# A hybrid RWKV-7 decoder step on one core: the scaled key turned by transfers instead of identity products, and four groups of operations scheduled with priority

## The chip, the core and the metric

The kernel runs on one core of a Trainium2 chip. TensorE (PE in the profile) multiplies matrices into PSUM; its weight loads (PEld) overlap its products. VectorE (DVE), ScalarE (ACT) and GpSimd (POOL) do the rest of the arithmetic, and SyncE (SP) issues most of the transfers. Each engine takes its instructions in order, and an instruction that waits holds what is behind it on that engine. The metric is the device time of one execution in microseconds; lower is better.

## The reference

One layer of a decoder trunk, for 1024 prompt tokens and 8 sequences of 8 sample tokens (1088 columns in all), model width 1024, 8 heads of 64:

```python
h = rms_norm(x, norm_mix) * (1 + sc) + sh
P = h @ w_in                                  # 4352 columns: RWKV, pooling, two gates
def step(S, inp):                             # one token of the RWKV-7 state, per head
    r_t, w_t, k_t, v_t, kk_t, a_t = inp
    sa = einsum("bhvk,bhk->bhv", S, -kk_t)
    S = S * w_t + sa[..., None] * (kk_t * a_t) + v_t[..., None] * k_t
    return S, einsum("bhvk,bhk->bhv", S, r_t)
merged = sigmoid(g_r) * (o_r @ w_br_rwkv) + sigmoid(g_p) * (o_p @ w_br_pool)
x = x + gt * (merged @ w_out)
x = x + gt2 * (square(relu(h2 @ w_ff1)) @ w_ff2)
y = rms_norm(x, norm_final)
```

## The kernel before

Features lie on the partitions, tokens along the free dimension. The wide products are made of float32 operands split in two: a high half (`hi`, float32r) and the rest (`lo`), and three products, hi by hi, hi by lo and lo by hi (`mm3`, L415), stand for one.

**Weights.** `weights` (L391) asks SP for 128x512 floats (`wraw`, two buffers), ScalarE rounds them to `whi`, DVE takes the difference `wlo`; `whi` and `wlo` have two buffers each (four in the second part). From its 68th call on, every other difference is GpSimd's. `products` (L439) issues a job's products, calls `load` for the half of a block that comes two later (L466), and at a job's end hands its three PSUM banks to `consume` (L473): the dense eviction, ScalarE's copy into `px` for the columns of `w_in`, DVE's operations for `w_br` and `w_out`.

**The RWKV units.** The heads are taken in four pairs. `front` (L808) makes decays, keys and sums of a pair on DVE and ScalarE. The 1024 prompt tokens are 16 chunks of 64, in units 0 and 1 of eight chunks each; unit 2 holds the sample tokens. `ra` (L888) makes two halves of a unit's tile `ra`: `ra[:, :, 1, :]` is the scaled key, minus `kk` times the decay, and `ra[:, :, 0, :]` the scaled receptance. For unit 0 `front` calls it (L876), for the others `unit` (L929). `unit` (L919) makes the scores (products `bk` by `ra`, masked by DVE into `ab[..., 0:64]` and `at`), scales the sums `bk`, brings the value rows by eight transfers of 32x32 blocks (`swap`, L1008, and a DVE transpose into `uv`), turns the scaled key by 16 products with the identity into a PSUM bank that DVE copies into `at[:, :, 0, :]` (L978 to L988), and turns the scaled sums into `ab[..., 64:128]` by TensorE and ScalarE (L992 to L998). `inverse`, `level` and `affine` solve the triangular systems of a pair; `affine` is the first to read `at[:, :, 0, :]`. `chain` (L1140) then runs through the 16 chunks: two products add to a bank, DVE makes the next state `S` out of it (L1164), two more products follow.

**The order.** TensorE's order is fixed when the program is made. `Pace` runs the wide products as background (`stream`) and puts the generators `chains`, `heads`, `pools` and `or_rows` between them; each yields a condition (`need`: operands and a bank are ready by the model of the other engines in `Clocks`, whose L142 prices an operation by its size; `room`: DVE's backlog is short) and runs on when it holds. The order of the other engines, SP's issues among them, is made at the build by a list scheduler that simulates the program: of the instructions whose operands are ready it takes the one earliest in the program. Transfers of `swap` and `weights` go through SP alike.

The second part (`phase2`, L1524) has `w_br`, `w_out` and the MLP, whose weights go through `pair` (L1518) with other buffers.

Of the kernel before, what the change touches and what calls it, by code (L numbers as in the profile page):

```python
# [9 lines left out]
F32 = mybir.dt.float32  # L10
F32R = mybir.dt.float32r
BF16 = mybir.dt.bfloat16
AF = mybir.ActivationFunctionType
ALU = mybir.AluOpType
# [307 lines left out]
class K:  # L322
# [68 lines left out]
    def weights(self, src):  # L391

        nc = self.nc
        n = self.nw
        self.nw += 1
        wp, x = (self.p2, "x") if self.deep and n % 4 > 1 else (self.wp, "")
        raw = self.wp.tile([P, 512], F32, tag="wraw", bufs=WB[0], name=self.nm("wraw"))
        nc.sync.dma_start(raw, src)
        hi = wp.tile([P, 512], F32R, tag="whi" + x, bufs=WB[1], name=self.nm("whi"))
        lo = wp.tile([P, 512], F32R, tag="wlo" + x, bufs=WB[1], name=self.nm("wlo"))  # L400
        nc.scalar.activation(hi, raw, AF.Copy)
        (nc.gpsimd if n % 2 and n >= self.solo else nc.vector).tensor_tensor(lo, raw, hi.bitcast(F32), op=ALU.subtract)
        return [(hi[:, q * 128:(q + 1) * 128], lo[:, q * 128:(q + 1) * 128]) for q in range(4)]

    def split(self, t, src):
# [33 lines left out]
    def products(self, flat, W, load):  # L439
        for j, h, *qs in flat:  # L440
            if isinstance(j, Unit):
                yield from j.go(W.pop((id(j), h)))
                load()
                if j.after:
                    j.after()
                continue
            if not isinstance(j, Job):
                yield from j()
                continue
            if h == 0 and (not qs or qs[0] == 0):  # L450
                if not j.hold:
                    j.consume = j.begin()
                j.pss = [self.ps(t) for _, t in zip(j.chunks, j.tags)]
            w = W[id(j), h]
            if not qs or qs[-1] == 3:
                del W[id(j), h]
            last = len(j.halves) - 1
            xh, xl = j.xs()
            for q in qs or range(4):
                for (c0, n), ps in zip(j.chunks, j.pss):  # L460
                    self.mm3(ps[:, :n], w[q], col(xh[4 * h + q], c0, n), col(xl[4 * h + q], c0, n),
                             h == 0 and q == 0, h == last and q == 3)
                    yield
            if qs and qs[-1] < 3:
                continue
            load()  # L466
            if h == last:
                if j.hold:
                    while j.hold not in self.done:
                        yield "idle"  # L470
                    j.consume = j.begin()
                for (c0, n), ps in zip(j.chunks, j.pss):
                    j.consume(c0, n, ps)  # L473
                if j.after:
                    j.after()

# [411 lines left out]
    def ra(self, d, u):  # L888
# [2 lines left out]
        C = 8 if u < 2 else 1  # L891
        cs = slice(8 * u, 8 * u + C)
        ra = self.p1.tile([P, C, 2, 64], F32, tag=f"ra{C}", bufs=2 if u < 2 else 1, name=self.nm("ra"))
        d["qs"][u] = dict(ra=ra)
        if u < 2:
            nc.vector.scalar_tensor_tensor(ra[:, :, 1, :], cut(kk[:, :NPR])[:, cs], -1.0, ev[:, cs, 0:64], op0=ALU.mult, op1=ALU.mult)
            nc.vector.tensor_tensor(ra[:, :, 0, :], cut(r[:, :NPR])[:, cs], ev[:, cs, 1:65], op=ALU.mult)
        else:
            nc.vector.scalar_tensor_tensor(cut8(ra[:, 0, 1, :]), cut8(kk[:, NPR:NT]), -1.0, es[:, :, 0:8], op0=ALU.mult, op1=ALU.mult)
# [19 lines left out]
    def unit(self, f, d, u):  # L919
# [8 lines left out]
        if u:  # L928
            self.ra(d, u)  # L929
        tl = lambda tag, shape, n=2: self.p1.tile([P, C] + shape, F32, tag=f"{tag}{C}", bufs=n if prompt else 1, name=self.nm(tag))  # L930
        Q = dict(ab=tl("ab", [2, 128]), uv=tl("uv", [2, 64]), ra=d["qs"][u]["ra"])
        d["qs"][u] = Q
        ra, ab, uv = Q["ra"], Q["ab"], Q["uv"]
        if prompt:
            at = Q["at"] = tl("at", [2, 64])
# [39 lines left out]
        if prompt:  # L975
            for h, hs in enumerate(HB):
                nc.vector.transpose(uv[hs, :, h, :], rest[h])
        yield self.need(ra, *[] if prompt else [v[:, NPR:NT]])  # L978
        ps = self.ps("w")
        for i in range(C):  # L980
            for h, hs in enumerate(HB):
                os = HB[1 - h]
                if prompt:
                    self.mm(ps[os, i * 64:(i + 1) * 64], ra[hs, i, 1, :], ident[hs, hs], start=True, stop=True, tile_position=(hs.start, os.start))
                else:
                    self.mm(ps[hs, 0:64], v[hs, NPR:NT], ident[hs, hs], start=True, stop=True)
        if prompt:
            nc.vector.tensor_copy(at[:, :, 0, :], cut(ps))  # L988
        else:
            for h, hs in enumerate(HB):  # L990
                nc.scalar.activation(uv[hs, 0, h, :], ps[hs, 0:64], AF.Copy)
        for a in range(0, C, 4):  # L992
# [147 lines left out]
    def chain(self, f, d):  # L1140
# [4 lines left out]
        for u in range(2):  # L1145
# [9 lines left out]
            for i in range(8):  # L1155
# [5 lines left out]
                else:  # L1161
                    for hs in HB:
                        self.mm(pn[hs, at], ra[hs, i, 1, :], S[hs, :], start=False, stop=True, skip_group_check=True)
                    nc.vector.scalar_tensor_tensor(S1, S, end[:, c:c + 1], pn[:, at], op0=ALU.mult, op1=ALU.add)  # L1164
                    for hs in HB:
                        self.mm(py[hs, at], S[hs, :], ra[hs, i, 0, :], start=False, stop=True, skip_group_check=True)
                S = S1
# [920 lines left out]
def cut(t):  # L2088
    return t.rearrange("p (c j) -> p c j", j=64)
# [90 lines left out]
```

## Time and profile before

| | |
|---|---|
| runs shown | 1601.74 and 1603.80 us, median 1602.77 us |
| profiled execution | 1604.23 us, of which 1602.4 us from the first to the last instruction |
| PE, DVE, ACT, POOL busy | 96%, 69%, 41%, 9% of the span |
| mean granted TensorE clock | 0.99 |
| transfers | 290.32 MB, 181 GB/s |

The page cuts the span into 40 slices of 40 us; a digit is the busy share of a slice in tenths (9 is 90% or more), PEclk the clock that the throttle granted:

```profile
PE   4999999999998999999999999999999999999997
PEld 2898888988898879989998999999999999999997
DVE  4575758776876487547542697998767796666774
ACT  4454354455334544522222572222334344344651
```

The first slice holds the first loads and the norm; up to about 775 us run `w_in`, the RWKV units and the pooling branch, behind that `w_br`, `w_out` and the MLP. A matmul of the profile has a modelled end, so a TensorE that is busy all the time is not one at its peak. A row of the waits reads: engine, tile and line that waited, what it waited for, us in total, times, longest. In a row of the timeline the bracket at the end is the idle time of the engine just before the instruction, and what ended it; L187 and L358 are the helpers that record every operation of DVE, ACT, POOL and SP, and every product, so the tiles' names tell what a row is (`kct` holds the identity).

### The profile page before, as it was taken

The numbers are of one execution on the slowest core, as the hardware profiler recorded it, in microseconds if no ns is written. First come the engines' busy times: TensorE is split into PE (matmuls) and PEld (weight loads), VectorE is DVE, ScalarE is ACT, GpSimd is POOL, SyncE is SP. The second block draws the span as 40 slices with busy tenths as digits, with TensorE's granted clock in tenths as the row PEclk, the third lists the DMA queues.
The fourth block names the chain that finished last, engine by engine and source line by source line (L and its number), as shares of the span: only waits on it lengthen the run. The fifth ranks groups of instructions, "written<-read, shape, count | busy, mean of one in ns | idle before, by whom it ended". The sixth has DMA issues, their size and how long they took to land.

```text
span 1602.4 us, 34165 instructions
## 1 busy us (share of the span) xinstructions
PE 1544.8 (96%) x13851; PEld 1453.6 (91%) x13851; DVE 1097.8 (69%) x1932; ACT 662.7 (41%) x1286; POOL 139.1 (9%) x220
## 2 busy tenths in 40 slices
PE   4999999999998999999999999999999999999997
PEld 2898888988898879989998999999999999999997
DVE  4575758776876487547542697998767796666774
ACT  4454354455334544522222572222334344344651
POOL 0100100000000000012500120000000050000000
PEclk9999999999999999999999999999999999999999
DMA  9242523234333343855884555665345996664753
GB/s 343 89 134 76 181 84 112 93 127 133 101 122 104 113 125 106 322 180 186 310 295 162 183 198 170 237 212 200 139 151 213 387 365 196 213 200 142 234 192 119
DMA packets 137438, 290.32 MB, mean 181 GB/s; under 512 B 37920, under 2 KB 42016, under 8 KB 137280
## 3 DMA queue, kind: packets, MB, share of 16 engines
q1 hardware_dynamic: 129856, 266.75, 48.4%
q10 hardware_dynamic: 5360, 14.26, 2.6%
q0 software_dynamic: 2064, 7.13, 1.3%
q8 instruction: 109, 1.79, 0.5%
q14 instruction: 49, 0.40, 0.1%
HBM read 210.80 MB, written 77.28 MB: 180 GB/s over the span
## 4 chain that ended last, share of the span: by engine, by line
PE 76%; DVE 6%; DMA 4%; issue 2%; ACT 1%; SPq 1%; DVEq 0%; ACTq 0%
PE mm L358 50%; PE w L358 13%; PE wc L358 12%; DVE wt L187 1%; DVE hx L187 1%; DMA mg<-in_w_ff 1%; DMA wt<-d_x 1%; SPq L187 1%; DMA hid<-in_w_ada_mlp 1%; DVE wlo L187 1%; DMA hid<-in_w_ff 1%; PE w L389 0%; DVE hv L187 0%; ACT wt L187 0%; DMA uv<-d_x 0%
## 5 line engine op out<-in xcount | busy, mean ns | idle before, releaser
L358 PE MATMUL mm<-hx,whi 128*128 128x362 f32 (+2 forms) x2944 | 689.9, 322 | 6.4 <-ACT px L187 3.7
L358 PEld LDWEIGHTS mm<-hx,whi 128*128 128x128 f32 x2944 | 497.3, 190 | 29.2 <-issue 11.5
L358 PE MATMUL mm<-hx,wlo 128*128 128x362 f32 (+2 forms) x1472 | 463.7, 315 | 5.8 <-DVE wlo L187 5.8
L358 PEld LDWEIGHTS mm<-hx,wlo 128*128 128x128 f32 x1472 | 279.5, 190 | 6.6 <-DVE wlo L187 6.6
L358 PE MATMUL mm<-mg,whi 128*128 128x272 f32 (+2 forms) x1312 | 249.5, 289 | 0.5 <-DVE t L187 0.5
L358 PEld LDWEIGHTS mm<-mg,whi 128*128 128x128 f32 x1312 | 205.4, 188 | 5.1 <-issue 2.5
L358 PE MATMUL mm<-mg,wlo 128*128 128x272 f32 (+2 forms) x656 | 188.5, 287 | 0.0
L358 PE MATMUL wc<-hx,whi 128*128 128x272 f32 x896 | 170.4, 287 | 0.0
L358 PEld LDWEIGHTS wc<-hx,whi 128*128 128x128 f32 x896 | 140.3, 188 | 0.0
L187 ACT ACTIVATE whi<-hid 128x512 fp32r<-128x512 f32 x128 | 80.4, 630 | 144.6 <-PE mm L358 59.6
L358 PE MATMUL wc<-hx,wlo 128*128 128x272 f32 x448 | 128.9, 288 | 1.0 <-DVE wlo L187 1.0
L358 PEld LDWEIGHTS mm<-mg,wlo 128*128 128x128 f32 x656 | 123.5, 188 | 0.0
L187 DVE TENSOR_TENSOR wlo<-hid,whi 128x512 fp32r<-128x512 f32 x128 | 87.9, 688 | 48.5 <-ACT whi L187 47.9
L187 DVE TENSOR_TENSOR wlo<-wraw,whi 128x512 fp32r<-128x512 f32 x84 | 60.7, 724 | 68.1 <-ACT whi L187 64.6
L187 ACT ACTIVATE whi<-wraw 128x512 fp32r<-128x512 f32 x100 | 62.6, 627 | 94.0 <-PE mm L358 56.9
L358 PE MATMUL w<-hx,whi 128*128 128x272 f32 (+1 forms) x480 | 96.9, 296 | 0.0
L358 PEld LDWEIGHTS wc<-hx,wlo 128*128 128x128 f32 x448 | 84.2, 188 | 1.3 <-DVE wlo L187 1.2
L187 POOL TENSOR_TENSOR hx<-hx,rs 128x64 f32<-128x64 f32 x24 | 35.2, 1465 | 569.5 <-DMA mg<-in_w_ff 376.2
L358 PEld LDWEIGHTS mm<-mg,hx 128*128 128x128 f32 x576 | 72.9, 188 | 5.0 <-issue 5.0
L358 PEld LDWEIGHTS w<-hx,whi 128*128 128x128 f32 x480 | 77.0, 188 | 0.0
L358 PE MATMUL mm<-mg,hx 128*128 128x272 f32 (+2 forms) x576 | 75.5, 290 | 0.0
L187 ACT ACTIVATE px<-mm 128x362 f32<-128x362 f32 (+3 forms) x113 | 46.3, 435 | 60.7 <-PE mm L358 53.9
(275 smaller groups left out, 2312.7 us busy)
## 6 DMA issues: line engine op xcount, KB each, us to landing
t<-d_t SPq DMA_DIRECT2D x56, 544.0 KB, 4.9
hid<-in_w_ff SPq DMA_DIRECT2D x110, 256.0 KB, 3.8
d_t<-hx SPq DMA_DIRECT2D x102, 272.0 KB, 2.2
hid<-in_w_ff SPq DMA_DIRECT2D x42, 512.0 KB, 3.8
wraw<-in_w_in SPq DMA_DIRECT2D x68, 256.0 KB, 2.8
mg<-in_w_ff SPq DMA_DIRECT2D x58, 256.0 KB, 5.4
hid<-in_w_ada_mlp SPq DMA_DIRECT2D x24, 512.0 KB, 5.7
d_th<-px SPq DMA_DIRECT2D x22, 544.0 KB, 3.0
```

The lines of the kernel that those rows point to most:

```text
L187: return f(*a, **kw)
L358: return self.nc.tensor.matmul(out, lhsT, rhs, **kw)
```

## The change

The scaled key of units 0 and 1 is turned without TensorE. `ra` allocates the tile `ab` too, and as soon as the scaled key is made it asks SP for eight transfers (two calls of `swap`) that put its 32x32 blocks into their turned places in `ab[:, :, 0, 64:128]`, the halves of the partitions exchanged. Where `unit` had the 16 identity products, the wait ahead of them and DVE's copy out of PSUM, DVE now transposes within the blocks from there into `at[:, :, 0, :]`. ScalarE later writes the turned sums into the same columns of `ab`. Unit 2 keeps its products for the value rows.

Four groups of operations are put into a block `high_priority()`: the scheduler takes them ahead of all others as soon as their operands are ready. They are the two operations of the weights' splitting in `weights`, a job's evictions, and the state sum `S1` in `chain`. TensorE's order stands outside of this, and so do the loads' transfers.

```diff
@@ weights
-        nc.scalar.activation(hi, raw, AF.Copy)
-        (nc.gpsimd if n % 2 and n >= self.solo else nc.vector).tensor_tensor(lo, raw, hi.bitcast(F32), op=ALU.subtract)
+        with self.tc.high_priority():
+            nc.scalar.activation(hi, raw, AF.Copy)
+            (nc.gpsimd if n % 2 and n >= self.solo else nc.vector).tensor_tensor(lo, raw, hi.bitcast(F32), op=ALU.subtract)
@@ products
                 for (c0, n), ps in zip(j.chunks, j.pss):
-                    j.consume(c0, n, ps)
+                    with self.tc.high_priority():
+                        j.consume(c0, n, ps)
@@ ra
-        d["qs"][u] = dict(ra=ra)
+        ab = self.p1.tile([P, C, 2, 128], F32, tag=f"ab{C}", bufs=2 if u < 2 else 1, name=self.nm("ab"))
+        d["qs"][u] = dict(ra=ra, ab=ab)
         if u < 2:
             nc.vector.scalar_tensor_tensor(ra[:, :, 1, :], cut(kk[:, :NPR])[:, cs], -1.0, ev[:, cs, 0:64], op0=ALU.mult, op1=ALU.mult)
+            for h, hs in enumerate(HB):
+                self.swap(ab[HB[1 - h], :, 0, 64:128], ra[hs, :, 1, :])
             nc.vector.tensor_tensor(ra[:, :, 0, :], cut(r[:, :NPR])[:, cs], ev[:, cs, 1:65], op=ALU.mult)
@@ unit
-        Q = dict(ab=tl("ab", [2, 128]), uv=tl("uv", [2, 64]), ra=d["qs"][u]["ra"])
-        d["qs"][u] = Q
+        Q = d["qs"][u]
+        Q["uv"] = tl("uv", [2, 64])
...
-        yield self.need(ra, *[] if prompt else [v[:, NPR:NT]])
-        ps = self.ps("w")
-        for i in range(C):
+        if prompt:
+            nc.vector.transpose(at[:, :, 0, :], ab[:, :, 0, 64:128])
+        else:
+            yield self.need(v[:, NPR:NT])
+            ps = self.ps("w")
             for h, hs in enumerate(HB):
-                os = HB[1 - h]
-                if prompt:
-                    self.mm(ps[os, i * 64:(i + 1) * 64], ra[hs, i, 1, :], ident[hs, hs], start=True, stop=True, tile_position=(hs.start, os.start))
-                else:
-                    self.mm(ps[hs, 0:64], v[hs, NPR:NT], ident[hs, hs], start=True, stop=True)
-        if prompt:
-            nc.vector.tensor_copy(at[:, :, 0, :], cut(ps))
-        else:
+                self.mm(ps[hs, 0:64], v[hs, NPR:NT], ident[hs, hs], start=True, stop=True)
             for h, hs in enumerate(HB):
                 nc.scalar.activation(uv[hs, 0, h, :], ps[hs, 0:64], AF.Copy)
@@ chain
-                    nc.vector.scalar_tensor_tensor(S1, S, end[:, c:c + 1], pn[:, at], op0=ALU.mult, op1=ALU.add)
+                    with self.tc.high_priority():
+                        nc.vector.scalar_tensor_tensor(S1, S, end[:, c:c + 1], pn[:, at], op0=ALU.mult, op1=ALU.add)
```

## The prediction, made before the changed kernel was run

> **What bounds the kernel now.** I read the page's busy shares first, then the busy table over three stretches, then TensorE's waits from 30 to 775 us, which is the part with the RWKV units.
>
> ```profile
> PE 1544.8 (96%) x13851; PEld 1453.6 (91%) x13851; DVE 1097.8 (69%) x1932; ACT 662.7 (41%) x1286; POOL 139.1 (9%) x220
> ```
> ```profile
> 30.00:775.00 745.00, 719.25 (x7351) 646.73 (x7344) 502.45 (x905) 329.17 (x674) 67.46 (x144) 0.98 0.42 139
> 775.00:1602.40 827.40, 815.63 (x6460) 800.75 (x6458) 583.75 (x1012) 318.96 (x596) 68.81 (x61) 1.00 0.62 214
> ```
> ```profile
> PE wc L358 <- DVE S L187: 6.4, 5, 2.8
> PE mm L358 <- DVE wlo L187: 5.2, 2, 3.4
> PE mm L358 <- ACT px L187: 3.7, 3, 3.1
> ...
> PE mm L358 <- DVE px L187: 1.4, 1, 1.4
> ```
>
> TensorE (PE) sets the time in both parts: what is taken off its work, or off its waits, is taken off the end. (The columns after the length are busy time of PE, weight load, DVE, ACT and POOL, then the granted clock.) Between 30 and 775 us it is idle for 745.0 - 719.3 = 25.8 us, and 16.7 of that are these four rows (total, times, longest). After 775 us it is idle for 11.8 of 827.4 us; of the changed lines only the weights of `w_br` and `w_out` and their evictions work there. I take nothing there, and look for the whole effect in the first part.
>
> The granted clock makes a wait dearer than its row says. These are the first part's stretches of low clock:
>
> ```profile
> 123.00:130.00 7.00, 5.71 (x27) 5.09 (x28) 6.83 (x11) 1.46 (x3) 0.77 (x2) 0.55 0.49 147
> 403.00:407.00 4.00, 4.00 (x19) 2.77 (x17) 3.97 (x6) 2.06 (x4) 1.26 (x2) 0.57 0.48 173
> 488.00:495.00 7.00, 5.37 (x18) 5.37 (x19) 5.48 (x8) 1.80 (x4) 0.85 (x5) 0.57 0.33 117
> 574.00:581.00 7.00, 5.63 (x27) 3.39 (x28) 6.57 (x13) 2.70 (x6) 1.20 (x2) 0.52 0.25 66
> ```
>
> The lost share of the clock is 0.45 x 7 = 3.2 us, 0.43 x 4 = 1.7, 0.43 x 7 = 3.0 and 0.48 x 7 = 3.4: 11.3 us in all, nearly as much again as the waits that stand before them.
>
> **Part 1: the identity products go.** In each of the eight prompt units, 16 products of 64x64 turned the scaled key into PSUM, and a DVE copy fetched it.
>
> ```profile
> 138.36 0.49 PE L358 MATMUL mm<-hx,whi 128*128 128x364 f32 x2
> 138.69 0.33 PE L358 MATMUL mm<-hx,wlo 128*128 128x364 f32 x1
> 138.95 1.15 PE L358 MATMUL w<-kct,ra 64*64 64x64 f32 x32
> 140.03 0.60 PE L358 MATMUL mm<-hx,whi 128*128 128x362 f32 x2
> ```
> ```profile
> L358 PE MATMUL w<-kct,ra 64*64 64x64 f32 x256 | 9.2, 221 | 0.0
> ```
>
> Two dense products take 138.69 - 138.36 = 0.33 us, one 0.17. From the start of the last one before the group to the next one behind it are 140.03 - 138.69 = 1.34 us, so the group costs 1.17 us and eight of them 9.4; its own busy time, 9.2, agrees (256 records are 8 x 32). TensorE has other products ready all the while, so the whole 9.4 comes off. The order of TensorE's work is worked out by the planner when the program is made. With one group and one point of waiting less in each unit, all that follows the first unit is laid out anew, and no later wait need stand where the trace has it.
>
> DVE exchanges the copy for a transpose of 512 columns:
>
> ```profile
> L187 DVE COPY at<-w x8: 690/692/694, 140.1 to 620.3; 128x512 f32<-128x512 f32 x8
> ```
> ```profile
> L187 DVE STREAM_TRANSPOSE uv<-uv x16: 694/706/709, 109.8 to 583.9; 64x512 f32<-64x512 f32 x16
> ```
> ```profile
> L187 DVE STREAM_TRANSPOSE iv<-iv 128x512 f32<-128x512 f32 x16 | 16.2, 1048 | 0.0
> ```
>
> At the second row's duration that is 8 x (706 - 692) ns = 0.1 us, at the third's (columns taken apart one by one) 2.8 us. DVE is busy 67% of this part, which covers either: between 0 and 2.8 I take 0, since the second row has the same runs of 64 columns.
>
> **Part 2: eight transfers a unit are added** on SP's queue, 64 in all, of the shape of those that bring the value rows:
>
> ```profile
> L187 SPq DMA_DIRECT2D uv<-d_x x64: 303/448/1882, 104.0 to 575.3; - x64
> ...
> DMA to landing us min/median/max: 1.7/2.3/5.6
> ```
>
> At 0.45 us each the queue is held for 3.6 us a unit, 29 us over the whole part, and the last piece lands 3.6 + 2.3 = 5.9 us after the key is made. The transpose on DVE waits for it; behind the transpose ScalarE waits to write the turned sum rows into the columns that the transfers borrowed (`ab`, 64 to 128); and behind that on ScalarE wait the evictions. The shortest way that a unit has, the last one's:
>
> ```profile
> 607.08 0.68 DVE L187 SCALAR_TENSOR_TENSOR ra<-wt,e 128x512 f32<-128x512 f32 x1
> ...
> 611.47 0.42 DVE L187 TENSOR_TENSOR ab<-w,kct 128x256 f32<-128x256 f32 x1 [1.56 <-PE w L358]
> ...
> 620.30 0.69 DVE L187 COPY at<-w 128x512 f32<-128x512 f32 x1
> ```
>
> The key is there at 607.8, the last piece at 613.7, and the copy that the transpose replaces ran at 620.3: 6.6 us to spare, so the 5.9 us are hidden by the unit's own scores and turning of the sums. If that cover were gone, TensorE would lose what is over. Should the masked scores (611.47) be held until the pieces have landed, since they write the same buffer, DVE would stand 2.2 us in such a unit: 0 to 8.8 us over the four units 1, taken as 0, because they write other columns. What stands behind the requests on SP is the third rival.
>
> **Part 3: priority.** Three of TensorE's waits, and what lay on the other engines ahead of what it waited for:
>
> ```profile
> 571.06 0.69 DVE L187 TENSOR_TENSOR bk<-wt,wt 64x512 f32<-64x512 f32 x1
> ...
> 572.76 0.87 DVE L187 TENSOR_SCALAR bk<-wt,hp 128x576 f32<-128x576 f32 x1
> 574.43 0.69 DVE L187 TENSOR_TENSOR ra<-wt,e 128x512 f32<-128x512 f32 x1 [0.80 <-DMA wt<-d_x]
> 575.04 0.27 DVE L187 SCALAR_TENSOR_TENSOR S<-S,end,wc 128x64 f32<-128x64 f32 x1
> ```
> ```profile
> 575.37 0.48 PE L358 MATMUL wc<-S,ra 64*64 64x64 f32 x4 [2.77 <-DVE S L187]
> ```
> ```profile
> 120.50 0.62 ACT L187 ACTIVATE whi<-wraw 128x512 fp32r<-128x512 f32 x1
> ...
> 121.99 1.52 DVE L187 SCALAR_TENSOR_TENSOR bk<-wt,wt 64x576 f32<-64x576 f32 x2
> ...
> 123.55 0.69 DVE L187 TENSOR_TENSOR wlo<-wraw,whi 128x512 fp32r<-128x512 f32 x1
> ...
> 124.29 0.67 PE L358 MATMUL mm<-hx,wlo 128*128 128x364 f32 x1 [3.37 <-DVE wlo L187]
> ```
> ```profile
> 402.72 0.33 PE L358 MATMUL wc<-S,ra 64*64 64x64 f32 x4 [1.15 <-DVE S L187]
> ```
>
> At 571 to 575 us and at 122 us, work of the front of a head, which nobody needs at once, stands ahead of the state sum `S` and of the low half of a weight, which TensorE needs at once. The blocks reverse that. Such an operation still waits for the one in progress, some 0.7 us long: half of that for each of the five waits for `S` leaves 6.4 - 1.8 = 4.6 us of gain, and 0.6 for each of the two for `wlo` leaves 5.2 - 1.2 = 4.0. Of the evictions, the one on DVE (1.4) may gain 1.0. The row of 3.7 on ScalarE gains nothing: 3.1 of it are the next wait, which is for a buffer that DVE is still reading, not for a place in the queue.
>
> ```profile
> 489.10 1.20 ACT L187 ACTIVATE px<-mm 128x364 f32<-128x364 f32 x3 [1.61 <-DVE px L187]
> ```
>
> The clock behind the waits that go (3.2 + 1.7 + 3.4 = 8.3 us) I take at half, 4.1, between nothing and all of it, since a new order has thin stretches of its own. The Trainium skill (TensorE: Matmul & The Clock Gate, "The HAM clock gate") says that the clock halves after an idle window of about 3.4 us. By that rule only the gap of 3.37 us, among those that go, would have brought a drop, the clock term would be 1.6, and the sum 1585 to 1586; the trace disagrees, with 0.57 behind a wait of 1.15 us and 0.52 behind one of 2.77 us.
>
> What is late next: an eviction that is put first on ScalarE holds what is behind it until TensorE is done, and the buffer wait at 489 us stays. For one new wait of that size with its loss of clock I add 3.4 us.
>
> **Sum**, on the profiled execution's 1604.2 us (span 1602.4): -9.4 - 4.6 - 4.0 - 1.0 - 4.1 + 3.4 = -19.7, so 1584.5. The median of the runs shown, 1602.8, is 1.4 lower, which gives 1583.
>
> **Rivals.** First, the blocks bring nothing: the order of TensorE is laid out by a planner that does not know of priorities, and new waits take the place of the old. Then only part 1 is left: 1602.8 - 9.4 = 1593.4, and up to 1600 with two new waits of 3.4. For it: there are only seven waits in the two rows, so luck has a part in them. Against it: in both quoted queues the same front work is in the way. Chance 0.20.
>
> Second, all waits of the four rows go, with all of the lost clock, and nothing comes instead: 9.4 + 16.7 + 11.3 = 37.4, so 1565. Against it: the buffer wait. Chance 0.10.
>
> Third, on the other side, SP's queue. A transfer that is asked for as soon as the key is made stands at the head of SP until DVE has made it, and the loads of weights stand behind.
>
> ```profile
> SPq L187 <- DVE wlo L187: 440.6, 171, 18.7
> ...
> SPq L187 <- DVE S L187: 24.8, 5, 12.3
> ```
>
> SP does stand like that now, up to 18.7 us at one request. The Trainium skill (DMA: Bandwidth & Descriptors, "Anatomy of one DMA") has the same mechanism: a wait is served on the sequencer that issues, ahead of dispatch; these rows agree. Half a block of weights keeps TensorE for 36 products of 0.17 us, 6 us, and there are two buffers, so a load that is held some 6 us longer than now reaches TensorE. The price is then the 3.6 us of the eight requests and 3.2 of clock, 6.8 us a unit. From three units on (19.7 / 6.8 = 2.9) the gain is gone; five of the eight give 1583 + 34 = 1617, all eight 1637. Against it: as many requests of this kind already pass through SP, and the loads' own long wait is for `wlo`, which is to come sooner. Chance 0.08.
>
> **How the numbers follow.** The forecast has 0.62, with its own range from 1575 to 1593: the clock term at nothing or all is 4.1 either way, no new wait or two are 3.4, and upwards comes the mask's 2.2 in one unit. The range from 1570 to 1600 takes in the first rival and leaves out most of the second (below) and the third (above). A measurement of this kernel can tell about 2% from no change, that is below 1570.7 or above 1634.8: faster by that 0.08 (nearly all of the second rival), slower 0.02 (the third with all units), within it 0.90.
>
> **What would show it.** Right: no group of 256 identity products; a DVE transpose into `at`; TensorE's waits for `S` and `wlo` under 4 us together before 775 us, and fewer stretches at half clock there; the second part as long as before, 827 us. Wrong: TensorE waiting for `whi` or `wlo` behind a `wraw` load that was asked for late (third rival); ScalarE's copies into `ab` waiting for the transpose into `at`; or TensorE's waits as large in sum as before (first rival).

## The result and the profile after

The changed kernel takes 1625.48 us (1624.58 to 1626.38), the kernel before 1602.77: a ratio of 1.014 with an interval of 1.0115 to 1.0166. It is 22.7 us slower: less than the 2% that the prediction named as the limit of a change, but clear of the spread between runs, above the predicted range of 1570 to 1600 and on the other side of the forecast.

TensorE does less and is idle more. The first row is the page's busy share; then the busy table over the stretch up to the same point of the work as 775 us before, and over what follows (columns as before: length, busy PE, PEld, DVE, ACT, POOL, clock).

```profile
PE 1541.3 (95%) x13595; PEld 1450.2 (89%) x13595; DVE 1100.5 (68%) x1932; ACT 654.6 (40%) x1280; POOL 138.7 (9%) x220
```
```profile
30.00:797.30 767.30, 718.52 (x7127) 646.75 (x7118) 507.76 (x906) 321.16 (x668) 70.14 (x145) 0.97 0.42 138
797.30:1624.60 827.30, 812.91 (x6432) 797.30 (x6430) 581.16 (x1011) 318.93 (x596) 65.73 (x61) 0.99 0.62 213
```

The 256 identity products are gone (13851 - 13595), and a transpose of 0.71 us stands in the place of each copy:

```profile
L187 DVE STREAM_TRANSPOSE at<-ab x8: 694/708/712, 118.6 to 640.8; 128x512 f32<-128x512 f32 x8
```

The second part is as long as before, 827.3 against 827.4 us. The whole loss is in the first part: 767.3 us in place of 745.0, with TensorE idle for 767.3 - 718.5 = 48.8 us in place of 25.8. Its busy time hardly fell, though 9.2 us of products are gone. Part of this is likely the clock (0.97 in place of 0.98): two of the products `w<-px,plw` are busy for 0.78 us before and for 1.55 us behind a long wait, as rows further down show. How much that makes in all was not worked out. These are its waits from 30 to 797.3 us (total, times, longest):

```profile
PE w L358 <- issue: 19.8, 3, 17.3
PE wc L358 <- DVE S L187: 11.1, 8, 5.2
PE w L358 <- ACT wt L187: 4.0, 6, 2.1
PE mm L358 <- DVE wlo L187: 3.8, 2, 1.9
PE mm L358 <- DVE px L187: 2.5, 1, 2.5
```

The state sum, which the block was to put first, is waited for longer than before (11.1 against 6.4 us), `wlo` a little less (3.8 against 5.2). New is one wait of 17.3 us in the first row, which stood like this before:

```profile
PE w L358 <- issue: 1.7, 2, 0.9
```

"Issue" says that the profile shows no releaser, so what it is has to be read from the tiles. In the timeline of PE:

```profile
417.41 0.32 PE L358 MATMUL mm<-hx,wlo 128*128 128x364 f32 x1
435.08 2.16 PE L358 MATMUL w<-px,plw 128*128 128x364 f32 x3 [17.35 <-issue]
```

`w<-px,plw` is the product of the pooling branch's third group (`pools`, L786): its operand `z` is made on DVE out of evicted columns, by window sums in `pool_cols` (L729). First ACT's eviction of the columns, then DVE:

```profile
406.45 0.40 ACT L187 ACTIVATE px<-mm 128x298 f32<-128x298 f32 x1
```
```profile
410.68 1.23 DVE L187 TENSOR_TENSOR d<-px 128x1038 f32<-128x1038 f32 x1
...
415.75 1.22 DVE L187 TENSOR_TENSOR px<-d 128x1036 f32<-128x1036 f32 x1
...
423.58 1.22 DVE L187 TENSOR_TENSOR d<-px 128x1032 f32<-128x1032 f32 x1
...
424.98 0.27 DVE L187 SCALAR_TENSOR_TENSOR S<-S,end,wc 128x64 f32<-128x64 f32 x1
...
431.87 1.23 DVE L187 SCALAR_TENSOR_TENSOR px<-d,px 128x1024 f32<-128x1024 f32 x1
...
434.81 0.16 DVE L187 COPY px<-zf 128x7 f32<-128x7 f32 x1
```

The columns are there at 406.85; `z` is there at 434.97, 0.11 us before the product starts. In between no DVE row has idle time before it: the chain's operations stand between those of the next head's front. Before, the same three events lay so (ACT, DVE, PE):

```profile
419.75 0.42 ACT L187 ACTIVATE px<-mm 128x298 f32<-128x298 f32 x1
```
```profile
432.14 0.17 DVE L187 COPY px<-zf 128x7 f32<-128x7 f32 x1
```
```profile
437.48 0.78 PE L358 MATMUL w<-px,plw 128*128 128x364 f32 x2
```

There the columns were there at 420.17, when DVE had most of the front behind it, and TensorE reached the product 5.2 us after `z`. `z` itself is only 2.7 us later than before; it is TensorE that comes 20 us earlier to the product, at 435.08 - 17.35 = 417.73. Why the planner's model had `z` ready by then was not traced.

The clock goes down behind the wait (the busy table of after over three short stretches):

```profile
421.00:435.00 14.00, 0.00 (x0) 0.00 (x0) 13.83 (x24) 2.57 (x4) 1.82 (x3) 0.50 0.28 61
435.00:438.00 3.00, 2.92 (x6) 1.88 (x7) 0.60 (x1) 0.69 (x2) 0.00 (x0) 0.51 0.63 180
438.00:441.00 3.00, 3.00 (x76) 2.63 (x75) 0.82 (x2) 0.44 (x1) 0.00 (x0) 1.00 0.03 11
```

An idle TensorE loses nothing by a low clock, so the price of the low clock is, by an estimate from these rows, half of the three us from 435 to 438. The Trainium skill (TensorE: Matmul & The Clock Gate, "The HAM clock gate") gives some 3.4 us of sustained work until the full clock is back; these 3 us agree.

### The profile page after: what moved, and what is told of

Read it like the earlier page. It is cut to its first block, busy times and chain, and to the rows that moved or that the text cites. A ratio compares the mean times of both kernels' runs of the same rounds, so it can differ in the third digit from the quotient of the medians.

```text
span 1624.6 us, 33746 instructions
## 1 busy us (share of the span) xinstructions
PE 1541.3 (95%) x13595; PEld 1450.2 (89%) x13595; DVE 1100.5 (68%) x1932; ACT 654.6 (40%) x1280; POOL 138.7 (9%) x220
## 4 chain that ended last, share of the span: by engine, by line
PE 65%; DVE 8%; DMA 8%; issue 2%; ACT 2%; SPq 1%; POOL 0%; DVEq 0%; ACTq 0%; POOLq 0%
PE mm L358 44%; PE wc L358 12%; PE w L358 9%; DMA hid<-in_w_ff 3%; DVE wt L187 2%; DVE hx L187 1%; DVE hv L187 1%; DMA mg<-in_w_ff 1%; DVE wlo L187 1%; DMA hid<-in_w_ada_mlp 1%; SPq L187 1%; DVE bk L187 1%; DMA wt<-d_x 1%; DVE mg L187 1%; DMA t<-d_t 0%
```

## The experiments

Two theories at first: the layout of TensorE's order, made anew by the planner, costs (A), or the transfers on SP's queue do (B); a third, that the priority blocks themselves cost (C). Times are medians, ratios are to the kernel before on the same chip, with their intervals.

### One part at a time, and the order held

`swap_only` is the change without its three priority blocks, `prio_only` the kernel before with them:

```diff
@@ swap_only, three times (weights, products, chain)
-        with self.tc.high_priority():
+        with ExitStack():
```

> The change without the three priority blocks; TensorE's order is that of the changed kernel, product by product. Theory A (TensorE's order, laid out anew, is what costs): 1625 us, within 4 of the changed kernel. Theory B (the eight transfers a unit hold SP's queue): also 1625. Theory C (the blocks are what costs): 1593, that is 1602.8 less the 9.4 of the identity products.

> The kernel before with the three priority blocks alone; TensorE's order is that of before. Theories A and B: 1603 us, within 4 of before. Theory C: 1615 or more. The prediction's own part 3 (the blocks take away waits worth some 10 to 14 us): 1590.

`same_order` makes the change without the blocks, but lets the planner go on counting the identity products, the copy and their wait, and not the transfers and transposes. A `Ghost` has a place in the planner's model and no instruction. TensorE's order is then that of before, less the eight groups:

```diff
@@ same_order, ra
+            self.clocks.on = False
             for h, hs in enumerate(HB):
                 self.swap(ab[HB[1 - h], :, 0, 64:128], ra[hs, :, 1, :])
+            self.clocks.on = True
@@ unit
+        yield self.need(ra, *[] if prompt else [v[:, NPR:NT]])
         if prompt:
...
+            for i in range(C):
+                for h, hs in enumerate(HB):
+                    self.ghost(Ghost(name, HB[1 - h].start, 64, i * 64, [(1, 64)]), ra[hs, i, 1, :], ident[hs, hs])
...
+            self.clocks.on = False
             nc.vector.transpose(at[:, :, 0, :], ab[:, :, 0, 64:128])
+            self.clocks.on = True
```

> Transfers and transpose in place of the identity products, no blocks, and the planner made to account for the identity products as if they were still there, so that TensorE's order is that of before less the eight groups. Theory A: 1593 us (1602.8 less 9.4), at most 4 off. Theory B: 1615 or more, since the same 64 transfers go through the same queue. Theory C: 1593.

`ident_new_order` is the reverse: the planner counts transfers and transposes that are not there, and the identity products and the copy are put into the changed kernel's order:

```diff
@@ ident_new_order, unit (the transfers in ra are only planned)
-            nc.vector.transpose(at[:, :, 0, :], ab[:, :, 0, 64:128])
+            self.plan("vector", "transpose", at[:, :, 0, :], ab[:, :, 0, 64:128])
...
+            for i in range(C):
+                for h, hs in enumerate(HB):
...
+                    self.nc.tensor.matmul(ps[os, i * 64:(i + 1) * 64], ra[hs, i, 1, :], ident[hs, hs], start=True, stop=True, tile_position=(hs.start, os.start))
...
+            nc.vector.tensor_copy(at[:, :, 0, :], cut(ps))
```

> The reverse: the identity products and DVE's copy as before, no transfers, no blocks, but the planner made to account for the transfers and the transpose, so that TensorE's order is that of the changed kernel with the eight groups put in. Theory A: 1635 us (1625 plus 9.4), down to 1628 if some of the products fall into a wait. Theory B: 1603, since there are no transfers. Theory C: 1603.

| | us | ratio to before |
|---|---|---|
| swap_only | 1628.61 | 1.0164 (1.0137 to 1.0192) |
| prio_only | 1602.78 | 1.0004 (0.9989 to 1.0019) |
| same_order | 1601.03 | 0.9991 (0.9978 to 1.0005) |
| ident_new_order | 1651.94 | 1.0308 (1.0283 to 1.0332) |

The blocks bring nothing that can be told from zero (within 3 us by the interval), so C falls. In the waits of `prio_only` from 30 to 775 us the two rows that they were meant for stand nearly as they did, 6.4 and 5.2:

```profile
PE wc L358 <- DVE S L187: 5.5, 5, 1.9
PE mm L358 <- DVE wlo L187: 5.3, 2, 3.5
```

With transfers and transposes in both, the new order costs 1628.6 - 1601.0 = 27.6 us: A stands. But `same_order` gains 2 us at most and not the 9.4 of the products, so something else takes the rest. And in the new order the identity products cost 1651.9 - 1628.6 = 23.3 us more than the transfers and transposes in their place, where in the old order the same exchange is worth 2: put where the planner had left no room for them, they wait on TensorE until ScalarE (`iv`) has read a bank. The waits of `ident_new_order` have a row for it (L996 are the identity products), and the pooling product's wait is there too, with no such transfer in the kernel:

```profile
PE w L358 <- issue: 18.4, 2, 16.7
PE w L996 <- ACT iv L187: 13.3, 8, 1.8
PE wc L358 <- DVE S L187: 12.8, 8, 5.4
```

### The products without their replacement

`no_ident` leaves the transfers out of `same_order` and puts a copy of `ra` in the place of each transpose; the planner's entries stay:

```diff
@@ no_ident, against same_order
-                self.swap(ab[HB[1 - h], :, 0, 64:128], ra[hs, :, 1, :])
...
-            nc.vector.transpose(at[:, :, 0, :], ab[:, :, 0, 64:128])
+            nc.vector.tensor_copy(at[:, :, 0, :], ra[:, :, 1, :])
```

> The kernel same_order without its transfers and transposes: the turned scaled key is left out, at holds a plain copy of ra, in one copy on DVE in place of each transpose. TensorE's order is the one of before without the identity products. Theory C (cover: the identity products filled time in which DVE was late, so taking them away buys little, and the transfers cost nothing): same time as same_order, 1598 to 1603, with the wait on bk near 136 us still there. Rival T (transfers and transposes gave the other 7 of the expected 9 us back): 1592 to 1596, and the wait on bk and ACT px back at before's values.

Measured: 1592.14 us, ratio 0.9934 (0.9919 to 0.9949). The rival T holds: the products are worth 1602.4 - 1592.1 = 10.3 us, and what replaces them costs 1601.0 - 1592.1 = 8.9 (9.1 by the ratios to before). With this the loss can be laid out in one chain of kernels. The first product of the MLP with `mg` ends the first part in each of them; the row is that of the tile's group, "first to last start" behind the durations. In this order: before, `no_ident`, `same_order`, `swap_only`, the changed kernel.

```profile
L358 PE MATMUL mm<-mg,whi x1312: 274/287/395, 793.7 to 1580.4; 128*128 128x272 f32 x170, 128*128 128x288 f32 x9, 128*128 128x256 f32 x9
```
```profile
L367 PE MATMUL mm<-mg,whi x1312: 274/287/393, 783.1 to 1568.2; 128*128 128x272 f32 x170, 128*128 128x288 f32 x9, 128*128 128x256 f32 x9
```
```profile
L367 PE MATMUL mm<-mg,whi x1312: 274/287/395, 791.8 to 1576.1; 128*128 128x272 f32 x170, 128*128 128x288 f32 x9, 128*128 128x256 f32 x9
```
```profile
L358 PE MATMUL mm<-mg,whi x1312: 274/287/393, 815.8 to 1601.2; 128*128 128x272 f32 x170, 128*128 128x288 f32 x9, 128*128 128x256 f32 x9
```
```profile
L358 PE MATMUL mm<-mg,whi x1312: 274/287/432, 816.0 to 1602.0; 128*128 128x272 f32 x170, 128*128 128x288 f32 x9, 128*128 128x256 f32 x9
```

793.7 to 783.1: the products go, -10.6. To 791.8: transfers and transposes come, +8.7. To 815.8: the order is laid out anew, +24.0. To 816.0: the blocks, +0.2 (by the medians -3.1, with intervals that overlap). The sum is +22.3; the two profiled spans differ by 1624.6 - 1602.4 = 22.2.

### What the transfers do: the queue of SP, in part

Where `same_order` loses the most at one place can be seen on three engines. SP, then DVE, then PE:

```profile
107.97 5.32 SPq L187 DMA_DIRECT2D ab<-ra  x8
113.34 2.08 SPq L187 DMA_DIRECT2D uv<-d_x  x4
...
118.09 5.31 SPq L187 DMA_DIRECT2D ab<-ra  x8
...
127.70 3.29 SPq L187 DMA_DIRECT2D uv<-d_x  x3
```
```profile
135.00 0.71 DVE L187 STREAM_TRANSPOSE uv<-uv 64x512 f32<-64x512 f32 x1 [4.16 <-DMA sw<-in_g]
...
138.01 1.23 DVE L187 TENSOR_TENSOR bk<-bk,end 128x1024 f32<-128x1024 f32 x1
```
```profile
139.39 0.63 PE L407 MATMUL w<-kct,bk 128*128 128x128 f32 x4 [3.13 <-DVE bk L187]
```

In `no_ident` the twelve requests for the value rows stand together, and the same product runs without a wait:

```profile
107.04 6.33 SPq L187 DMA_DIRECT2D uv<-d_x  x12
```
```profile
137.76 0.60 PE L407 MATMUL w<-kct,bk 128*128 128x128 f32 x4
```

Two blocks of eight requests for the key, 5.3 us each, go ahead of the value rows; their last request goes out at 131 us in place of 113, DVE stands 4.16 us at the transpose that needs them, and behind it on DVE wait the masks and the scaled sums that TensorE wants. (The releaser named, `sw`, is only the transfer that landed last before.) It is the third rival's engine and queue, but it was not the weights that came late: the waits for `wlo` are 3.5 us here and 4.6 in `no_ident`.

Three kernels ask where the cost goes when the requests are taken off SP, or DVE's wait for them is taken away. `swap_idle` leaves the turned key out, as `no_ident` does, but keeps the transfers:

```diff
@@ swap_pool, against same_order (swap_act: self.nc.scalar)
-                self.swap(ab[HB[1 - h], :, 0, 64:128], ra[hs, :, 1, :])
+                self.swap(ab[HB[1 - h], :, 0, 64:128], ra[hs, :, 1, :], self.nc.gpsimd)
@@ swap_idle, against same_order
-            nc.vector.transpose(at[:, :, 0, :], ab[:, :, 0, 64:128])
+            nc.vector.tensor_copy(at[:, :, 0, :], ra[:, :, 1, :])
```

> The kernel same_order with the key's 64 transfers asked for on the queue of GpSimd instead of SP; TensorE's order unchanged. Theory S (SP's queue: near 108 and 118 us two blocks of eight requests, 5.3 us each, stand ahead of those for the value rows, whose last go out at 127.7 to 131.0 us, DVE stands 4.16 us at the uv transpose behind them and TensorE waits 3.1 us for bk): the wait on bk falls under 1.5 us, the first product of the feed-forward comes at 784 to 787 us in place of 791.8, and the time is 1592 to 1597, under before's by more than 5. Theory D (DVE standing at the transposes for the landing, and the transposes being longer than a copy): it stays at 1599 or more, and as the requests land later, it may be above 1605.

> The same with the transfers asked for on ScalarE's queue. Theory S: SP is as free as in swap_pool, but ScalarE's queue is in order and holds evictions, which stand behind eight requests of some 0.6 us: 1594 to 1601, with TensorE's waits on ACT (px, wt, hv, iv) up by 2 to 5 us. Theory D: 1600 or more, with DVE's waits on ab from ra as in same_order, 6 us.

> The kernel same_order with the 64 transfers on SP as they are, but the turned key left out of at: a copy of ra on DVE takes the place of each transpose, so nothing on DVE waits for the landing (the copies into ab's columns still do). Theory S: nearly all of the 9 us stays, 1598 to 1602, with DVE's late uv near 131 us still there. Theory D: 1592 to 1595, as no_ident.

| | us | ratio to before | first product with `mg` |
|---|---|---|---|
| swap_pool | 1599.80 | 0.9979 (0.9964 to 0.9995) | 788.1 |
| swap_act | 1603.47 | 1.0006 (0.9987 to 1.0026) | 791.3 |
| swap_idle | 1600.06 | 0.9989 (0.9972 to 1.0005) | 790.0 |

`swap_idle` decides between the two theories: no engine's waits have a row for the landing there, and yet 7.9 of the 8.9 us stay (6.9 of 8.7 in the profiled runs), and DVE stands 4.82 us at the value rows there, now with their own name:

```profile
133.92 0.71 DVE L187 STREAM_TRANSPOSE uv<-uv 64x512 f32<-64x512 f32 x1 [4.82 <-DMA uv<-d_x]
```

So most of it comes with the transfers being asked for, and not with DVE's wait for the landing. But `swap_pool` falls short of what the queue theory said. The wait on `bk` is gone and the first part is 3.7 us shorter than in `same_order`, on a queue that asks faster (eight requests in 4.65 us against 5.32 on SP):

```profile
107.07 4.65 POOL L187 DMA_DIRECT2D ab<-ra  x8 [4.95 <-DVE ra L187]
```

Yet the time falls by 1.2 us only, not to 1592 to 1597, and in the profiled run the second part is longer (788.1 to the last product at 1577.8, 789.7 us, where `same_order` has 784.3); why was not tried. Of the first part's 8.7 us, 5.0 stay as well (788.1 against the 783.1 of `no_ident`), though here too no engine is seen to wait for the landing. So SP's queue is shown for 3.7 of the 8.7 us, and the cause of the rest stays open. ScalarE's queue is no better: 1603.47 us where the queue theory expected 1594 to 1601, with TensorE's waits on ACT `px` at 11.4 us in place of 4.8. The Trainium skill (DMA: Bandwidth & Descriptors, "Issuing engines are not separate DMA queues") says that asking from several engines saves only the time on the sequencer, which is usually small beside the transfer; here one request holds SP for a median of 0.61 us, less than the 1.9 us until it lands, but eight in a row hold it for 5.3 us. `swap_pool` is the one version with nothing left out that is clear of the kernel before, by two thousandths of it.

### What the new order does: TensorE ahead of DVE

`late_pool` is the changed kernel with the three chunks of the pooling product, their evictions and their transfers, which the planner still counts where it did, written 20 us of planner time later. Nothing else in TensorE's order moves:

```diff
@@ late_pool, pools
                 yield self.need(z[:, c0:c0 + m], plw, zs, wait=0, spare=6000)
+                if g == 2:
+                    self.planned(hi, lo, plw, z, zs, c0, n, m)
+                    continue
...
+            if g == 2:
+                self.done.add(("op", g))
+                yield Later(self.pace, self.pace.t + 20000)
...
+                    self.mm(ps[:, :m], plw, z[:, c0:c0 + m], start=True, stop=True)
```

> The changed kernel with one thing moved: in the pooling branch's third group (g=2) the planner still counts the three chunks' products and evictions where it puts them now, but they are written into the queues 20 us of planner time later; TensorE's order is otherwise the one of the changed kernel, instruction by instruction. Theory P (most of the loss is this one product put ahead of its operand): the wait of 17.35 us before w<-px,plw goes, TensorE's waits on issue fall from 19.8 to under 4 us, with a part of the lost clock at 420.9 us, and the time falls by 16 to 22 us, to 1604 to 1610. Theory Q (the wait only stands in for DVE's backlog, so the next product that needs DVE waits as long instead): the time falls by less than 6 us, to 1620 or more, and another wait of 10 us or more stands between 417 and 450 us.

`no_pool_dve` leaves TensorE's order wholly alone and takes DVE's chain away instead, so that the products read the columns as they were evicted (GpSimd clears the small tile `zs`):

```diff
@@ no_pool_dve, pool_cols
+            dve = Planned(self.clocks, "vector") if g == 2 else nc.vector
...
-            nc.vector.scalar_tensor_tensor(z, s[:, 15:W], 1.0 / win, z, op0=ALU.mult, op1=ALU.subtract)
+            dve.scalar_tensor_tensor(z, s[:, 15:W], 1.0 / win, z, op0=ALU.mult, op1=ALU.subtract)
```

> The changed kernel, which leaves out the vector engine's chain of window sums and z of the pooling branch's third group (g=2; some 7 us of DVE work between 410.68 and 434.81 us); its products read the evicted columns instead. The planner still counts the chain, so TensorE's order is the changed kernel's, instruction by instruction. Theory P+Q together (DVE has 28 us of work back to back after these evictions, and the chain stands in the middle of the next head's front: TensorE's order is harmless wherever DVE isn't late): the 17.35 us wait goes altogether, and the state sum that late_pool still waited 6.0 us for comes earlier too, to under 4 us: 1603 to 1609. Theory O (TensorE's order itself is worse, whatever DVE does): the wait goes, others of over 10 us in sum come: 1612 or more, as late_pool's 1614.

Measured: `late_pool` 1614.11 us, ratio 1.0074 (1.005 to 1.0098), 11.4 below the changed kernel; `no_pool_dve` 1613.48, ratio 1.0067 (1.0044 to 1.009), 12.0 below. In the profiled executions the first product with `mg` comes at 807.3 and 798.8 in place of 816.0, 8.7 and 17.2 us earlier. In `late_pool` 6 us of the wait came back at once, in the form that theory Q gave it though smaller. This row of the PE timeline shows where; the next is DVE's:

```profile
426.11 1.97 PE L381 MATMUL wc<-ab,uv 128*64 128x64 f32 x32 [5.99 <-DVE S L187]
```
```profile
425.79 0.27 DVE L187 SCALAR_TENSOR_TENSOR S<-S,end,wc 128x64 f32<-128x64 f32 x1
```

It is the state sum that stood in the same DVE backlog at 424.98 in the changed kernel, hidden there behind the longer wait. So both theories hold a part: the pooling product was ahead of its operand, and behind it DVE was late for the next thing as well. With 7 us of DVE's work away, as `no_pool_dve` has it, that wait too is gone from the place (2.79 us stand there, for a bank that DVE reads into `hv`), and 17.2 of the 24.0 us of the order are gone in the profiled run. That run, 1607.66 us, is the shortest of its kernel (the longest is 1617.16), so by the medians about half of the loss is explained by this one collision, by the profile some three quarters. Both are upper bounds, since the 7 us of DVE's work were not taken out of the kernel before for comparison.

Neither time fell where it was expected. `late_pool` lies between the ranges of P and Q. `no_pool_dve` lies by its median in the range of theory O, 1612 or more, and by its profiled run in that of P and Q together; the further waits of over 10 us that O asks for are not there, as TensorE is idle for 38.1 us from 30 us to the first product with `mg`, where the changed kernel has 51.9. What the rest of the new order costs it is open.

### How much a draw of the order is worth

The planner's order hangs on constants. Three of them were moved a little, in the kernel before and in the changed one; nothing is added or removed:

```diff
@@ before_170, after_170 (mm and tr, a change between tile sizes)
-            self.pace.t += 150 if self.clocks.on else 200
+            self.pace.t += 170 if self.clocks.on else 200
@@ before_800, after_800 (chain, margin of a state sum)
-                    yield self.need(S, banks=(), wait=LS[f], spare=700)
+                    yield self.need(S, banks=(), wait=LS[f], spare=800)
@@ before_7000, after_7000 (pools)
-                yield self.need(z[:, c0:c0 + m], plw, zs, wait=0, spare=6000)
+                yield self.need(z[:, c0:c0 + m], plw, zs, wait=0, spare=7000)
```

> The kernel before with one estimate of the planner changed by 20 ns (the price of a change between tile sizes on TensorE, 150 to 170 ns) and no instruction added or removed: the same work in another order. Theory L (the time depends on the layout by 10 us and more): the time moves by over 5 us from 1603, and the sum of TensorE's waits on S, issue, ACT and DVE moves with it. Rival M (layouts of the same work agree within 5 us, and the change's loss has a cause of its own): 1598 to 1608.

> The changed kernel with the same estimate changed by 20 ns. Theory L: the layout differs from 1002 products on, the pooling product lands elsewhere, and the time moves by over 5 us from 1625, more likely down since the wait of 17 us is a rare one: 1600 to 1618. Rival M (something that the transfers and the missing products bring in any layout): 1620 to 1630.

> The kernel before with the planner's margin for a state sum raised from 700 to 800 ns; no instruction added or removed, the same work in another order. Theory L (each layout draws its own waits; before's happens to be a good one): slower by 2 to 15 us, 1605 to 1618. Rival M (layouts of the same work agree within 5 us): 1598 to 1608. Where both hold, before_170's 1606.6 counts as well.

> The changed kernel with the same margin raised from 700 to 800 ns. Theory L: another draw, 1600 to 1625; if its pooling product again comes before z, 1618 to 1626, if not, 1600 to 1614. Rival M (the changed kernel is slower in every layout by the same amount): 1620 to 1630.

> The kernel before with the planner's margin for all pooling products raised from 6000 to 7000 ns; the same work in another order. Theory L (the loss is a matter of the draw): anywhere in 1598 to 1622, with no wait of 10 us or more in one place. Theory Y (systematic: only the changed kernel's planner runs ahead of DVE): under 1616, as the two draws so far, 1606.6 and 1614.6.

> The changed kernel with the same margin raised from 6000 to 7000 ns. Theory Y: 1616 to 1632, with a wait of 10 us or more before w<-px,plw near 417 us, since 1 us of margin is small beside the 17. Theory L: 1600 to 1616.

| constant | work of before, us (ratio to before) | work of the change, us (ratio to before) |
|---|---|---|
| as it was | 1602.77 | 1625.48 (1.0115 to 1.0166) |
| 150 to 170 | 1606.55 (1.0012 to 1.0057) | 1621.67 (1.0089 to 1.0141) |
| 700 to 800 | 1614.57 (1.0061 to 1.0095) | 1636.06 (1.0182 to 1.0217) |
| 6000 to 7000 | 1619.63 (1.008 to 1.0121) | 1617.65 (1.0073 to 1.0108) |

The same work of the kernel before takes from 1602.8 to 1619.6 us, by nothing but its order: 17 us, three quarters of the change's loss. The order that the change started from is the fastest of its four. The means are 1610.9 and 1625.2, but in the last pair the sign turns, and four draws with a spread of 17 and 18 us don't settle how much of the 14 between the means belongs to the change. One thing does: the wait before the pooling product is in all four draws of the changed kernel. In `after_170`, `after_800` and `after_7000`:

```profile
437.29 1.55 PE L358 MATMUL w<-px,plw 128*128 128x364 f32 x2 [17.28 <-issue]
```
```profile
431.43 1.55 PE L358 MATMUL w<-px,plw 128*128 128x364 f32 x2 [15.06 <-issue]
```
```profile
433.92 1.55 PE L358 MATMUL w<-px,plw 128*128 128x364 f32 x2 [14.37 <-issue]
```

None of the four of before has it; `before_7000`, the slowest, loses its time in many places, the longest of them 4.5 us. The expectations came out mixed. The smallest shift stayed within rival M's ranges in both kernels (1606.55 and 1621.67); `before_800` and `before_7000` moved as theory L has it, and `before_7000` is above theory Y's 1616; `after_800` is above both of its ranges; `after_7000` is within Y's, with the wait that Y names.

`pool_spare` gives that product a margin of 24000 ns (g=2 alone) and lets the planner lay out what follows; `both_fixes` asks for its transfers on GpSimd as well:

```diff
@@ pool_spare, pools (both_fixes: and swap on self.nc.gpsimd)
-                yield self.need(z[:, c0:c0 + m], plw, zs, wait=0, spare=6000)
+                yield self.need(z[:, c0:c0 + m], plw, zs, wait=0, spare=(24000 if g == 2 else 6000))
```

> The changed kernel with the planner's margin for the same product raised from 6000 to 24000 ns (g=2 alone), so that the planner itself puts it later and lays out anew all that follows on TensorE. Theory P: the wait of 17.35 us goes and what follows is no worse, 1602 to 1612. Theory Q: 1620 or more. Theory L (each new layout draws its own waits, whatever was meant): the 17 us go, but others of 5 us or more come or go elsewhere, anywhere from 1598 to 1630.

> The changed kernel with the margin of the third pooling group at 24000 ns, as in pool_spare, and the key's transfers asked for on GpSimd's queue, as in swap_pool; TensorE's order is pool_spare's. If the two causes add up: 1614.1 less the 2 to 4 us that swap_pool gained on same_order, 1609 to 1613, still slower than before, since the order's other waits (S 14.5 us in pool_spare) are untouched. If they account for the whole loss: 1603 or less.

Measured: 1614.10 us, ratio 1.007 (1.0044 to 1.0095), and 1618.80, ratio 1.0091 (1.0064 to 1.0118). The margin takes the same 11 us off that `late_pool` does, which is 2 us short of theory P and within L's range. The queue of GpSimd adds nothing to it: both intervals overlap, and the expected 1609 to 1613 was missed. In this order the waits for `S` are 14.5 and 14.7 us against 6.4 in the kernel before.

## Why the prediction was wrong, step by step

**Part 1, the identity products, -9.4: right.** In an order that is otherwise held, leaving them out gave -10.3 (`no_ident`).

**Part 2, transfers and transposes at nothing: wrong.** They cost 8.9 us (8.7 in the profiled runs). The prediction looked for the cover of the landing, at the last unit, and there TensorE shows no new wait in `same_order`; `swap_idle` shows that the landing is at most a small part of the price. What it left out was the request's place in SP's queue beside the value rows, which go through the same queue for the same unit: that is 3.7 of the 8.7 us by `swap_pool`, and the other 5.0 stay open. The request was also taken too short, at 0.45 us from the value rows' transfers; it measures a median of 0.61, and the first eight take 5.3 us in place of 3.6. The third rival had the queue, but behind it the weights, at a price of 6.8 us a unit, 54 for all eight units.

**Part 3, the priority blocks, -9.6 and half of the lost clock, -4.1: wrong.** `prio_only` gives 1.0004 (0.9989 to 1.0019). Front work stood ahead of `S` and `wlo` in DVE's queue, as quoted, but the blocks leave it there. In `prio_only` `whi` is ready at 121.67 us, and two more operations of the front still go first on DVE:

```profile
121.05 0.62 ACT L187 ACTIVATE whi<-wraw 128x512 fp32r<-128x512 f32 x1
...
122.68 1.52 DVE L187 SCALAR_TENSOR_TENSOR bk<-wt,wt 64x576 f32<-64x576 f32 x2
...
124.23 0.69 DVE L187 TENSOR_TENSOR wlo<-wraw,whi 128x512 fp32r<-128x512 f32 x1
```

TensorE's waits for `S` and `wlo`, which were to be under 4 us together, are 14.9 us in the changed kernel. The lost clock was also priced a little high: it was taken over the whole stretches, and counted over TensorE's busy time alone, as an idle TensorE loses nothing, the four rows give 9.3 us in place of 11.3. That the scheduler chooses only among operations that are ready by its own simulated time, where TensorE waits at other places than on the chip, is an explanation that was not tried.

**The sum's "For one new wait of that size with its loss of clock I add 3.4 us": the step that decided.** The prediction has "all that follows the first unit is laid out anew" two parts earlier, and then prices it as one wait. It measures 24.0 us at the end of the first part (`swap_only` against `same_order`), one wait of 17.35 among it. The kernel's own spread over orders, 17 us for the same work, was not in the range either; with it 1600 could not have been the upper end.

**The first rival was right in its mechanism, wrong in its size.** The blocks bring nothing, the order is laid out anew, and new waits take the place of the old; but 1593.4 to 1600 held only two waits of 3.4 us, and the identity products' gain was taken to stay, where the transfers and transposes take 8.9 of its 10.3 us back.

**Right besides:** the transpose's duration (0.71 us), no second-part effect (827.3 against 827.4 us), and the last of the signs named under "wrong": TensorE's waits as large in sum as before. They were larger.

## What to carry to other kernels

When a program's order is planned, price an edit in the old order and the new layout as two terms: hold the order (let the planner count what is no longer there) and the edit's own worth can be measured by itself. Take the spread of a few neighbouring orders of the unchanged program as the least width of any range. An engine that is busy for two thirds of the span can still need 28 us at one place to deliver 7 us of work, so a new order of the bounding engine can run it into the backlogs of the others; and a small transfer has to be priced by what stands behind its request in the queue, not only by its landing.

## What the runs showed of the hardware that was not expected

One request of 32 KB for the key holds its queue for a median of 0.61 us on SP, 0.58 on GpSimd and 0.62 on ScalarE, with median landings of 1.9, 2.1 and 2.1 us. The first eight in a row hold SP for 5.3 us and GpSimd for 4.65: asking for eight takes longer than one takes to land, and for these transfers GpSimd asks no slower than SP.

Runs of one program differ by 10 us and more, and the granted clock goes along with it only in part: of the ten of `swap_act` the fastest (1598.62 us) has a clock of 0.994 and the slowest (1609.29) 0.987, but four at 0.990 or 0.991 lie anywhere from 1598.89 to 1604.90. A difference of a few us between two programs is therefore read from medians, or from the place of one product in two profiles whose clocks agree.
